# One 512-byte remainder for all large tiles, the attention output split into the buffer of the normed activations, and plain products in the last piece of each MLP, in a two-layer f32 encoder

## The chip, the cores and the metric

The kernel runs on one core of a Trainium2 chip. The metric is device time in microseconds (us) of one execution; a lower time is better. Times before are 1498.27, 1499.73 and 1499.77, median 1499.73.

## The reference

An input `x` of 512 tokens by 1024 goes through two layers. Each layer has a token mixer and an MLP, each behind an RMS norm and added to the residual:

```python
for i in range(DEPTH):                       # DEPTH = 2
    h = rms_norm(x, norm_mix[i])
    if i % 2 == 0:
        y = dilated_mixer(h, a_w_qkv[j], a_q_gain[j], a_k_gain[j], a_w_o[j])
    else:
        y = mla_mixer(h, b_w_in[j], b_q_a_gain[j], b_w_qb[j], b_kv_a_gain[j], b_w_kvb[j], ...)
    x = x + y
    h = rms_norm(x, norm_ffn[i])
    x = x + sq_relu_mlp(h, ffn_w1[i], ffn_w2[i])   # relu(h @ w1)**2 @ w2, 1024 -> 4096 -> 1024
```

Mixer A (layer 0) is windowed attention in three groups of dilation 1, 4 and 16, with 8 heads of 128 each; the three outputs of a head are merged by their softmax denominators, and a 1024 x 1024 output projection follows. Mixer B (layer 1) projects to latents of 256 (queries), 128 (keys and values) and 64 (rotary key), expands them to 8 heads, attends over all 512 tokens and has an output projection of the same size. Everything is f32.

## The kernel before, in words

**Three products for one.** TensorE multiplies in the rounded form fp32r. Each f32 operand is split into a high part (rounded) and a low part (the rest), and a product is the sum of high x high, high x low and low x high. A weight unit of 256 rows by 512 columns comes by DMA from SyncE's queue (SP) into a `raw` tile (3 buffers, line 130); ScalarE copies it to `whi` (L145), VectorE subtracts to get `wlo` (L146), 4 buffers each. Activations are split the same way: `hT` holds the normed activations transposed, high and low, in 32 KB of each partition. Such tiles come from the pool `big` under the tag "hT" (`new_hT`). `run_block` (L149 to L178) is the ordinary block: four accumulators in PSUM, the weight units one after another or all four loaded first, the three products at L172, and a function `evac` for each finished accumulator.

**Stages in order.** Norm of the input; mixer A, two heads at a time; output projection (`project`, L620); MLP; norm; mixer B; projection; MLP; store.

**Mixer A.** For each pair of heads the loop from L436 makes queries, keys and scores (`qk_all`; probabilities are the tiles `P`), values (`v_all`), then `merge` (L364 to L405) and `pv` (L407 to L434). `merge` brings maxima and denominators of the first group into the order of the others by small products with a selection matrix (L374), works out the weights on VectorE and ScalarE, brings them back by another product (L399) and multiplies all `P` tiles with them (L405). `pv` transposes `P` (L117), multiplies with the values (L428, L432) and copies to `oT`. For the last pair the order is values of head 0, `qk_all`, `merge`, values of head 1, `pv` twice.

**Mixer B.** One pair of heads at a time: scores (L829), softmax, transposed probabilities in `pTs` (L845 and its neighbour), value product (`pv_b`, L853) and a ScalarE copy to `oB`. The heads are staggered by three token rows. For the last pair all PSUM tiles come from the pools `sc` and `tp` (`bank`, L734), so that the four accumulators are free.

**Output projection.** `project` splits `oT` or `oB` into two tiles `osp` (L626 to L628, eight copies on ScalarE and eight subtractions on VectorE, after the attention), then multiplies in two halves of 512 columns, 96 products each; in the second half each finished row is normed (`norm_tile`) and its transposed, split form goes to `hT` (L117, L208, L209).

**MLP.** Four pieces of 1024 hidden units. An up block is 96 products (L172); the activations `a2` are f32. A down piece (`wino`, L470) multiplies 2 x 2 blocks with seven block products in place of eight: 7 x 24 = 168 matmuls, with sums and differences of activation blocks (tile `S`) and of weight blocks (tiles `wq`) on VectorE (L493), splits of both (L502 and L503 to `asp`, L509 and L510 to `whi` and `wlo`), and results added to the residual (L545). The order is up(0,0), up(0,1), then for each piece up(ch+1,0), down(ch), up(ch+1,1), and down(3) at the end. `ORDER` and `ORDER_P` list the seven products; the last piece of each MLP uses `ORDER_P`, which finishes rows earlier, and calls `done` after each step: norms in layer 0, stores in layer 1.

**What sets the order.** The program runs under a tile framework whose scheduler reorders each engine's instructions by a simulated timeline, within the dependences; on the chip each engine then runs its list in that order. Pools give the addresses, and a tile of a pool waits until the readers of what stood there are done.

**Addresses.** In the built program the tiles start at these remainders of their byte address in the partition modulo 512:

| tiles | before | after |
|---|---|---|
| hT, raw, whi, wlo, pTs | 192 | 192 |
| oT, oB, the a2 in `x16`, osp, resid, wq, asp, S, mixer A's P of group 0 and its constants | 64 | 192 (osp is gone) |
| mixer A's other tiles (values, keys, tables, pT) | 352 | 192 |
| mixer B: kn, kr, vb | 384 | 192 |
| mixer B: qn, qr, pe | 448 | 192 |
| mixer B: latents cT and rotary tables | 96 | 192 |

Of the kernel before, what the change touches and what calls it, by code (L numbers as in the profile page):

```python
# [10 lines left out]
F32 = mybir.dt.float32  # L11
# [6 lines left out]
P = 128  # L18
# [36 lines left out]


# [29 lines left out]
def encoder_kernel(ctx: ExitStack, tc: tile.TileContext, x, norm_mix, norm_ffn, a_w_qkv, a_q_gain, a_k_gain,  # L86
# [17 lines left out]
    st = ctx.enter_context(tc.tile_pool(name="st", bufs=6))  # L104
    acc_p = ctx.enter_context(tc.tile_pool(name="acc_p", bufs=4, space=PSUM))
# [123 lines left out]
    with tc.tile_pool(name="apool", bufs=1, reuse_waits="tile") as ap_, \  # L229
            tc.tile_pool(name="aw", bufs=2, reuse_waits="tile") as aw, \  # L230
            tc.tile_pool(name="adram", bufs=2, space=bass.MemoryType.DRAM) as ad:
        xts = [aw.tile([P, D], F32, tag="vt", name=nm("xt")) for r in range(2)]
# [8 lines left out]
        ca = ap_.tile([P, C_ALL - C_KEEP], F32, name="ca")  # L241
        gqk = ap_.tile([P, 2, NG * DH], F32, name="gqk")
        load_x(0)
# [24 lines left out]
        cosg, sing = {}, {}  # L268

        def tables(g):  # L270
            eng = V if g == 0 else G
            cg = ap_.tile([P, NT, 2, DH], F32, name=f"cosg{g}")
            sg = ap_.tile([P, NT, 2, DH], F32, name=f"sing{g}")
# [5 lines left out]
            cosg[g], sing[g] = cg, sg  # L279
# [156 lines left out]
        for b in range(HA // 2):  # L436
# [33 lines left out]
    def wino(tag, Aq, w, pool, resid, order, done=None):  # L470
# [29 lines left out]
        def split_a(x):  # L500
            t = pool.tile([P, 4, 2, 256], F32R, tag="asp", name=nm("asp"), bufs=3)
            A.activation(t[:, :, 0], x, AF.Copy)  # L502
            V.tensor_tensor(t[:, :, 1], x, t[:, :, 0].bitcast(F32), op=ALU.subtract)  # L503
            return t

# [7 lines left out]
        def need_t1():  # L513
            if "t1" not in raw:
                sub(b11, b12, b11)
                raw["t1"] = b11

        def operands(p):
            if p == 1:
                return Aq(0, 0), b11  # L520
            if p == 5:
                stmp("c", Aq(1, 0), Aq(1, 1), ALU.add)
                need_t1()
# [8 lines left out]
            if p == 7:  # L532
                stmp("d", Aq(0, 0), Aq(1, 0), ALU.subtract)
                need_t1()
# [13 lines left out]
        for step, (p, chain, first, last, adds) in enumerate(order):  # L548
            a, wq = operands(p)
            at = split_a(a)  # L550
# [394 lines left out]
```

## Time and profile before

| quantity | value |
|---|---|
| median of three runs | 1499.73 us |
| profiled execution | 1500.14 us |
| its span (first to last instruction) | 1498.4 us |
| mean granted TensorE clock | 0.981 of full speed |
| TensorE busy | 1436.6 us, 7116 matmuls |
| VectorE busy | 954.1 us |
| ScalarE busy | 723.6 us |
| GpSimd busy | 176.8 us |
| DMA, mean over the span | 90 GB/s |

The profile is that of one execution. Its own time, 1500.14 us, is 1.7 us more than its span, for what lies ahead of the first and behind the last instruction. Times of stages are read from the span, in us from its start. PE is TensorE, DVE VectorE, ACT ScalarE, POOL GpSimd and SP SyncE; a line number such as L172 is one of the code above. A row of the timeline has start, busy time, engine, line, operation, output and inputs, tile and element counts, and in square brackets an idle time ahead of it with what ended it. "x8" means that so many instructions were put together.

### The profile page before, as it was taken

The page shows a single profiled execution, that of the slowest core. Times are in us where ns is not written, and L with a number is a line of the kernel's source. Part 1 is how long each engine was busy: PE and PEld are TensorE (multiplying, and loading weights), DVE is VectorE, ACT ScalarE, POOL GpSimd, SP SyncE. Part 2 cuts the span into 40 slices and gives each one's busy share as a digit, 9 for nine tenths or more (in the row PEclk, how much of TensorE's full clock was granted, in tenths as well). Part 3 has the DMA queues.
Part 4 walks back from the last instruction along what each step waited for, and adds up shares of the span by engine and source line. Part 5 has one row for each costly group of instructions (what it writes and reads, how often), then busy time and mean ns, then how long its engine had stood idle before and what let it go on. Part 6 is the DMA issues. An engine that isn't in the chain of part 4 may idle for free.

```text
span 1498.4 us, 19268 instructions
## 1 busy us (share of the span) xinstructions
PE 1436.6 (96%) x7116; PEld 1211.0 (81%) x7116; DVE 954.1 (64%) x1386; ACT 723.6 (48%) x1566; POOL 176.8 (12%) x301
## 2 busy tenths in 40 slices
PE   5999999999999799999999997899889999999997
PEld 4889889889988788888888886777668888888885
DVE  5675565656447634484866877587745286675966
ACT  3653455355336423554535444587633453544542
POOL 5210120120012100000000001664300000000000
PEclk9999999999999899999999998899999999999998
DMA  6315214313422334415151501210003515151401
GB/s 224 92 54 154 69 52 134 96 47 90 139 85 81 96 112 149 147 57 154 29 169 43 163 1 41 64 43 29 29 29 111 184 30 168 42 169 56 127 0 56
DMA packets 112334, 135.44 MB, mean 90 GB/s; under 512 B 7409, under 2 KB 71537, under 8 KB 112241
## 3 DMA queue, kind: packets, MB, share of 16 engines
q1 hardware_dynamic: 112240, 134.22, 29.0%
q8 instruction: 56, 0.92, 0.3%
q14 instruction: 38, 0.30, 0.1%
HBM read 130.00 MB, written 4.19 MB: 90 GB/s over the span
## 4 chain that ended last, share of the span: by engine, by line
PE 87%; DVE 7%; ACT 3%; issue 1%; DMA 1%; POOL 1%; SPq 0%; DVEq 0%; ACTq 0%; POOLq 0%
PE acc L172 55%; PE sc L563 10%; PE tp L563 8%; PE tp L117 3%; PE acc L853 1%; PE sc L746 1%; DVE wlo L510 1%; PE acc L829 1%; DVE wlo L146 1%; PE sco L428 1%; DVE resid L545 1%; PE sco L432 1%; PE sc L339 1%; PE acc L563 1%; PE tp L853 1%
## 5 line engine op out<-in xcount | busy, mean ns | idle before, releaser
L172 PE MATMUL acc<-whi,hT 128*128 128x512 f32 (+2 forms) x1344 | 403.2, 376 | 0.7 <-ACT hT L208 0.7
L146 DVE TENSOR_TENSOR wlo<-raw,whi 128x1024 fp32r<-128x1024 f32 (+3 forms) x172 | 198.7, 1162 | 268.0 <-ACT whi L145 261.7
L172 PE MATMUL acc<-hT,whi 128*128 128x512 f32 (+1 forms) x1152 | 321.9, 366 | 2.4 <-DVE resid L639 1.9
L145 ACT ACTIVATE whi<-raw 128x1024 fp32r<-128x1024 f32 (+3 forms) x172 | 171.7, 1001 | 296.3 <-PE acc L172 221.9
L172 PEld LDWEIGHTS acc<-whi,hT 128*128 128x128 f32 x1344 | 248.6, 190 | 30.5 <-ACT hT L208 1.2
L172 PE MATMUL acc<-wlo,hT 128*128 128x512 f32 (+2 forms) x672 | 250.1, 373 | 2.6 <-DVE wlo L146 2.6
L172 PEld LDWEIGHTS acc<-hT,whi 128*128 128x128 f32 x1152 | 208.4, 189 | 37.9 <-DVE resid L639 2.2
L509 ACT ACTIVATE whi<-wq 128x1024 fp32r<-128x1024 f32 x112 | 118.6, 1061 | 193.4 <-PE acc L172 77.8
L172 PE MATMUL acc<-hT,wlo 128*128 128x512 f32 (+1 forms) x576 | 208.1, 365 | 0.0
L510 DVE TENSOR_TENSOR wlo<-wq,whi 128x1024 fp32r<-128x1024 f32 x112 | 136.9, 1222 | 63.6 <-ACT whi L509 62.9
L563 PE MATMUL sc<-whi,asp 128*128 128x512 f32 x480 | 155.1, 395 | 0.0
L172 PEld LDWEIGHTS acc<-wlo,hT 128*128 128x128 f32 x672 | 127.3, 189 | 18.5 <-DVE wlo L146 3.6
L563 PE MATMUL tp<-whi,asp 128*128 128x512 f32 x352 | 118.0, 407 | 10.6 <-DVE asp L503 6.4
L172 PEld LDWEIGHTS acc<-hT,wlo 128*128 128x128 f32 x576 | 108.6, 189 | 17.6
L563 PEld LDWEIGHTS sc<-whi,asp 128*128 128x128 f32 x480 | 90.4, 188 | 21.0
L563 PE MATMUL sc<-wlo,asp 128*128 128x512 f32 x240 | 94.4, 395 | 0.0
L563 PEld LDWEIGHTS tp<-whi,asp 128*128 128x128 f32 x352 | 68.7, 196 | 29.0 <-DVE asp L503 7.9
L172 PE MATMUL acc<-whi,osp 128*128 128x512 f32 x256 | 80.5, 395 | 1.2 <-ACT osp L627 1.2
L493 DVE TENSOR_TENSOR wq<-wq,wq 128x1024 f32<-128x1024 f32 x64 | 77.7, 1222 | 0.9
L563 PE MATMUL tp<-wlo,asp 128*128 128x512 f32 x176 | 71.2, 404 | 0.0
L122 POOL TENSOR_SCALAR rs_v<-qss 128x4 f32<-128x4 f32 (+1 forms) x64 | 22.7, 354 | 396.2 <-ACT junk L291 363.7
L122 POOL TENSOR_SCALAR rs_v<-nss 128x1 f32<-128x1 f32 x16 | 5.3, 330 | 530.5 <-ACT xn L198 530.5
(193 smaller groups left out, 2120.2 us busy)
## 6 DMA issues: line engine op xcount, KB each, us to landing
raw<-in_ffn_w_dram SPq DMA_DIRECT2D x64, 512.0 KB, 3.7
wq<-in_ffn_w_dram SPq DMA_DIRECT2D x64, 512.0 KB, 4.4
raw<-in_a_w_qkv_dram SPq DMA_DIRECT2D x96, 256.0 KB, 3.1
raw<-in_a_w_qkv_dram SPq DMA_DIRECT2D x64, 192.0 KB, 2.8
raw<-in_a_w_o_dram SPq DMA_DIRECT2D x8, 512.0 KB, 4.7
raw<-in_b_w_o_dram SPq DMA_DIRECT2D x8, 512.0 KB, 3.7
xt<-in_x_dram SPq DMA_DIRECT2D x8, 256.0 KB, 5.7
vd<-vt SPq DMA_DIRECT2D x8, 256.0 KB, 3.8
```

The source lines that it names most:

```text
L117: PE.transpose(o, i, ident)
L122: G.tensor_scalar(v[:, :n], ss, 1.0 / dim, EPS, op0=ALU.mult, op1=ALU.add)
L145: A.activation(hi[:, :nk, :n], raw[:, :nk, :n], AF.Copy)
L146: V.tensor_tensor(lo[:, :nk, :n], raw[:, :nk, :n], hi[:, :nk, :n].bitcast(F32), op=ALU.subtract)
L172: PE.matmul(accs[o][:, oc], lhsT=lt, rhs=rt, start=(kt == 0 and p_i == 0 and hv == 0), stop=(kt == total - 1 and p_i == 2), skip_group_che ...
L339: PE.matmul(sc[:, r * P:(r + 1) * P], lhsT=qT[:, r * P:(r + 1) * P], rhs=kT[:, r * P:(r + 1) * P], start=True, stop=True)
L428: PE.matmul(o[:, r * P:(r + 1) * P], lhsT=vt[:, r, g], rhs=pts[g - 1][:, r * P:(r + 1) * P], start=(r == 0 and g == 1), stop=False, skip_g ...
L493: V.tensor_tensor(o[u], x[u], y[u], op=ALU.subtract)
L509: A.activation(hi, x, AF.Copy)
L510: V.tensor_tensor(lo, x, hi.bitcast(F32), op=ALU.subtract)
L563: PE.matmul(bk[t], lhsT=lt, rhs=rt[:, j], start=(first and k == 0 and i == 0), stop=(k == 3 and i == 2), skip_group_check=True)
L853: PE.matmul(o, lhsT=d["v"][:, j, h], rhs=pT[:, j], start=(j == 0), stop=(j == NT - 1))
```

## The change

It has three parts and some consequences.

1. *Remainders.* Small tiles (`gn`, `ssr`, `rqs`) move to a pool `sm` with a pad of 128 f32; the constants `ca` and the tile `kr2` are widened; `ck` and mixer A's tables are allocated in another place. All large tiles then start at remainder 192 (table above).
2. *Attention output.* Its split form now lies in a tile of `big` in the slot of "hT": in mixer A `oA`, taken after the last `v_all`, with the same eight copies and eight subtractions; in mixer B `oB`, into which `pv_b` writes the high part (ScalarE) and the low part (VectorE) straight from PSUM, so that the later copies and subtractions are gone. `pTs` goes to `x16`. The normed activations of the MLPs get tiles of their own (`hT_f0`, `hT_f1`).
3. *Last piece of each MLP.* `down_last` replaces the seven products by an ordinary block of eight: four splits of `a2` and 2 x 96 = 192 products at the line of `run_block`, with the weights loaded and split like all others. Each row and half is finished by itself and calls `done(r, c)`: in layer 0 the norm of row r when its second half is finished, in layer 1 a store. `ORDER_P` is gone.
4. The weights of the inner seven-product pieces lie in one tile `wqs` in the slot of "hT"; `asp` has 4 buffers in place of 3; the two loads of `gn` are issued early on SP's queue.

```diff
+    sm = ctx.enter_context(tc.tile_pool(name="sm", bufs=1))
+    gn = sm.tile([P, 2], F32, name="gn")
+    ssr = sm.tile([P, NT], F32, name="ssr")
+    rqs = [sm.tile([P, NT, 2], F32, name=f"rqs{i}") for i in range(2)]
+    sm.tile([P, PAD], F32, name="pad")
...
+        cas = ap_.tile([P, 1920], F32, name="ca")
+        ca = cas[:, 0:C_ALL - C_KEEP]
...
                 merge(stats, Pt, True)
                 vs.append(v_all(1))
+                oA = new_hT()
...
-                t = pool.tile([P, 2, 512], F32, tag=f"wq{slot}", name=nm("wq"), bufs=2)
+                t = wqs[:, 2 * slot + u]
...
+        wqs = big.tile([P, 8, 2, 512], F32, tag="hT", name=nm("wqs"))
...
+        def down_last(ch):
+            a2 = a2s.pop(ch)
+            at = {}
+            for j in range(2):
+                for i in range(2):
+                    at[i, j] = split_a(a2[:, 4 * j:4 * j + 4, 256 * i:256 * i + 256], pool)
+            def mm(r, kt, hi, lo, hv):
+                t = at[r // 2, kt // 4][:, kt % 4]
+                ah, al = (t[:, c, (r % 2) * P:(r % 2) * P + P] for c in range(2))
+                sl = slice(0, 512)
+                return [(ah, hi, sl), (ah, lo, sl), (al, hi, sl)]
+            for c in range(2):
+                def evac(r, acc, c=c):
+                    sl = resid[:, r, 512 * c:512 * c + 512]
+                    V.tensor_tensor(sl, sl, acc, op=ALU.add)
+                    done(r, c)
+                run_block(w_units(w2[1024 * ch:1024 * ch + 1024, :], 512 * c, 512), [1] * 4 if c == 0 else [4], 512,
+                          mm, evac)
...
-        down(3)
+        down_last(3)
-    def project(oS, w, resid, gain_src, pool, g_name):
+    def project(o_hl, w, resid, gain_src, hT_n, pool, g_name):
...
-        parts = [pool.tile([P, 4, 2, S], F32R, name=nm("osp")) for _ in range(2)]
-        for h in range(8):
-            o_hl = parts[h // 4][:, h % 4]
-            A.activation(o_hl[:, 0], oS[:, h], AF.Copy)
-            V.tensor_tensor(o_hl[:, 1], oS[:, h], o_hl[:, 0].bitcast(F32), op=ALU.subtract)
...
+        for h in range(HA):
+            A.activation(oA[:, h, 0], oT[:, h], AF.Copy)
+            V.tensor_tensor(oA[:, h, 1], oT[:, h], oA[:, h, 0].bitcast(F32), op=ALU.subtract)
+        project(oA, a_w_o[0], resid, norm_ffn[0:1, :].rearrange("o d -> (o d)"), hT, po, "g_ffn0")
...
-                A.activation(oB[:, hh], o, AF.Copy)
+                A.activation(oB[:, hh, 0], o, AF.Copy)
+                V.tensor_tensor(oB[:, hh, 1], o, oB[:, hh, 0].bitcast(F32), op=ALU.subtract)
...
-            oB = x16.tile([P, HB, S], F32, tag="x16", name="oB")
-            pTs = big.tile([P, 2, NT, S], F32, tag="hT", name="pTs")
+            oB = new_hT()
+            pTs = x16.tile([P, 2, NT, S], F32, tag="x16", name="pTs")
```

The scheduler gives TensorE another order at three places. Rows show line, operation, output and inputs, and shape; numbers tell tiles of one name apart.

The first place is the merge of mixer A's last pair of heads. `sc` is the last score, `scm` the merge's small products, `P` the probabilities, `sco` the value product. Before:

```order
L339 MATMUL sc_4666<-qkT_4433 128x128
L374 MATMUL scm_4681<-ca,xsel_4678 128x4 x4
L399 MATMUL scm_4702<-ca,xsel_4678 128x4 x2
L117 MATMUL tp_4858<-ck,P_3774 128x128 x4
L117 MATMUL tp_4865<-ck,P_3776 128x128 x4
L428 MATMUL sco_4886<-pT_4863,vt_3782 128x128
L117 MATMUL tp_4872<-ck,P_3772 128x128 x4
```

After, TensorE has products of the output projection there (`hT_4866` is `oA`, `acc_4995` to `acc_4998` are the projection's four accumulators):

```order
L179 MATMUL acc_4998<-whi_5001,hT_4866 128x512
L179 MATMUL acc_4998<-wlo_5002,hT_4866 128x512
L381 MATMUL scm_4689<-ca,xsel_4686 128x4 x4
L179 MATMUL acc_4995<-whi_5001,hT_4866 128x512 x2
L179 MATMUL acc_4995<-wlo_5002,hT_4866 128x512
```

Some rows on, around the merge's second small product:

```order
L179 MATMUL acc_4998<-wlo_5062,hT_4866 128x512
L179 MATMUL acc_4998<-whi_5061,hT_4866 128x512 x2
L179 MATMUL acc_4998<-wlo_5062,hT_4866 128x512
L406 MATMUL scm_4710<-ca,xsel_4686 128x4 x2
L124 MATMUL tp_4867<-ck,P_3782 128x128 x4
L124 MATMUL tp_4874<-ck,P_3784 128x128 x4
L179 MATMUL acc_4998<-whi_5061,hT_4866 128x512
L124 MATMUL tp_4881<-ck,P_3780 128x128 x4
```

Between the last score and `scm_4710` there were the four small products alone; now 71 products of the projection's first half stand there too.

The second place is the end of the first MLP with its norms (`xn` is a normed row, `acc_7796` an accumulator of mixer B's input projection). Before:

```order
L563 MATMUL sc_7394<-wlo_7705,asp_7685 128x512
L563 MATMUL sc_7394<-whi_7704,asp_7685 128x512
L117 MATMUL tp_7647<-ck,xn_7640 128x128 x4
L117 MATMUL tp_7654<-ck,xn_7640 128x128 x4
L172 MATMUL acc_7796<-whi_7802,hT_7638 128x448
```

After (`acc_7504` is the last row's accumulator, `xn_7558` the first normed row):

```order
L179 MATMUL acc_7504<-whi_7507,asp_7364 128x512
L124 MATMUL tp_7565<-ck,xn_7558 128x128 x4
L124 MATMUL tp_7572<-ck,xn_7558 128x128 x4
L179 MATMUL acc_7504<-wlo_7508,asp_7364 128x512
L179 MATMUL acc_7504<-whi_7507,asp_7364 128x512 x2
```

The transposes of the first row stood behind the last product of the MLP; now they stand among the products of its last row.

The third place is the end of mixer B (`pTs`, `vb`: value product; `pe`: probabilities to be transposed; `kn`, `qn`, `kr`, `qr`: scores). Before:

```order
L853 MATMUL tp_9697<-pTs,vb_9191 128x512 x4
L117 MATMUL tp_9716<-ck,pe_9649 128x128 x4
L829 MATMUL sc_9703<-kn_9189,qn_9552 128x512 x3
L829 MATMUL sc_9703<-kr_9190,qr_9553 128x512 x2
L117 MATMUL tp_9722<-ck,pe_9668 128x128 x4
L117 MATMUL tp_9728<-ck,pe_9687 128x128 x4
L117 MATMUL tp_9734<-ck,pe_9712 128x128 x4
L853 MATMUL tp_9740<-pTs,vb_9191 128x512 x4
L172 MATMUL acc_9772<-whi_9778,osp_9754 128x512
```

After (`hT_7969` is `oB`, `acc_9715` and `acc_9716` are accumulators of the projection):

```order
L179 MATMUL acc_9715<-whi_9750,hT_7969 128x512
L838 MATMUL sc_9550<-kn_9143,qn_9495 128x512 x3
L838 MATMUL sc_9550<-kr_9144,qr_9496 128x512 x2
L124 MATMUL tp_9589<-ck,pe_9521 128x128 x4
L179 MATMUL acc_9715<-whi_9750,hT_7969 128x512
L179 MATMUL acc_9715<-wlo_9751,hT_7969 128x512
```

The projection began behind the last value product; now 84 of the first half's 96 products stand ahead of it, between the scores and transposes of the last pair.

More of the change, by code (lines that the diff above doesn't have):

```diff
@@ L54 @@
 C_KEEP = C_COSA
+PAD = 128
 def shape_constants():
@@ L231, in encoder_kernel @@
             tc.tile_pool(name="adram", bufs=2, space=bass.MemoryType.DRAM) as ad:
+        cosg = [ap_.tile([P, NT, 2, DH], F32, name=f"cosg{g}") for g in range(NG)]
+        sing = [ap_.tile([P, NT, 2, DH], F32, name=f"sing{g}") for g in range(NG)]
         xts = [aw.tile([P, D], F32, tag="vt", name=nm("xt")) for r in range(2)]
@@ L467, in encoder_kernel, with split_a, wino @@
                 pv(b, h, Pt, *vs[h])
-    def wino(tag, Aq, w, pool, resid, order, done=None):
+    def split_a(x, pool):
+        t = pool.tile([P, 4, 2, 256], F32R, tag="asp", name=nm("asp"), bufs=4)
+        A.activation(t[:, :, 0], x, AF.Copy)
+        V.tensor_tensor(t[:, :, 1], x, t[:, :, 0].bitcast(F32), op=ALU.subtract)
+        return t
+    def wino(tag, Aq, w, wqs, pool, resid):
         v = w.rearrange("(k p) c -> p k c", p=P)
@@ L511, in split_w @@
             return hi, lo
[L513 to L516, printed above, removed]
         def operands(p):
@@ L547, in wino @@
         banks = {}
-        for step, (p, chain, first, last, adds) in enumerate(order):
+        for p, chain, first, adds in ORDER:
             a, wq = operands(p)
-            at = split_a(a)
+            at = split_a(a, pool)
             if first:
-                pl, tg = {"a": (sc_p, "sc"), "b": (tp_p, "tp"), "d": (acc_p, "acc") if order is ORDER_P else (tp_p, "tp")}[chain]
+                pl, tg = (sc_p, "sc") if chain == "a" else (tp_p, "tp")
                 banks[chain] = [pl.tile([P, 512], F32, tag=tg, name=nm(tg)) for _ in range(2)]
@@ L607, in down @@
             a2 = a2s.pop(ch)
-            last = ch == 3
             wino(layer * 4 + ch, lambda i, j: a2[:, 4 * j:4 * j + 4, 256 * i:256 * i + 256],
-                 w2[1024 * ch:1024 * ch + 1024, :], pool, resid, ORDER_P if last else ORDER, done if last else None)
+                 w2[1024 * ch:1024 * ch + 1024, :], wqs, pool, resid)
+        def down_last(ch):
[16 more added lines that the diff above has]
+                          mm, evac)
         up(0, 0)
@@ L899, in encoder_kernel @@
                     tail = fresh
+    bh = ctx.enter_context(tc.tile_pool(name="bh", bufs=1, reuse_waits="tile"))
+    hT = bh.tile([P, KD, 2, S], F32R, name="hT_f1")
     with tc.tile_pool(name="po1", bufs=1, reuse_waits="tile") as po:
[L902 removed]
+        project(oB, b_w_o[0], resid, norm_ffn[1:2, :].rearrange("o d -> (o d)"), hT, po, "g_ffn1")
     with tc.tile_pool(name="mlp1", bufs=1, reuse_waits="tile") as mp:
[L905 to L912 removed]
+        mlp(1, ffn_w1[1], ffn_w2[1], hT, resid, mp, lambda r, c: nc.sync.dma_start(
+            out_v[:, r, 512 * c:512 * c + 512], resid[:, r, 512 * c:512 * c + 512]))
 _INS = ['x', 'norm_mix', 'norm_ffn', 'a_w_qkv', 'a_q_gain', 'a_k_gain', 'a_w_o', 'b_w_in', 'b_q_a_gain', 'b_w_qb',
```

65 lines of the change are left out of this document (17 added, 48 removed).

## The prediction

> **What bounds the kernel now.** I read the page first: busy times, the clock in 40 slices, and the chain that ended last.
>
> ```profile
> span 1498.4 us, 19268 instructions
> ...
> PE 1436.6 (96%) x7116; PEld 1211.0 (81%) x7116; DVE 954.1 (64%) x1386; ACT 723.6 (48%) x1566; POOL 176.8 (12%) x301
> ...
> PEclk9999999999999899999999998899999999999998
> ...
> PE 87%; DVE 7%; ACT 3%; issue 1%; DMA 1%; POOL 1%; SPq 0%; DVEq 0%; ACTq 0%; POOLq 0%
> ```
>
> PE carries 87% of the chain. So time can come off in three ways only: fewer products, a shorter product, or fewer holes in PE's row and fewer stretches at a lower clock. The page's 96% hides the holes, so I cut the span into stages and asked for the busy time of each (columns: stretch, its length, then for each engine busy us and instructions, then the granted clock, DMA share, GB/s).
>
> ```profile
> 507.80:533.85 26.05, 17.25 (x107) 15.94 (x108) 13.06 (x31) 9.11 (x27) 0.00 (x0) 0.67 0.36 107
> 607.43:650.98 43.55, 43.55 (x194) 36.06 (x193) 26.34 (x23) 22.40 (x29) 0.00 (x0) 1.00 0.31 97
> 650.98:690.02 39.04, 39.04 (x169) 31.65 (x168) 33.39 (x35) 20.74 (x22) 0.00 (x0) 1.00 0.45 134
> 876.90:924.80 47.90, 42.84 (x169) 33.61 (x168) 40.11 (x43) 22.37 (x26) 2.45 (x4) 0.89 0.07 18
> 924.80:952.88 28.08, 25.09 (x129) 22.56 (x128) 14.55 (x19) 13.00 (x34) 7.60 (x16) 0.94 0.12 34
> 952.88:975.20 22.32, 16.63 (x73) 13.35 (x72) 14.40 (x46) 14.47 (x59) 17.39 (x40) 0.77 0.32 95
> 1071.00:1103.30 32.30, 24.83 (x100) 15.43 (x98) 17.68 (x48) 13.20 (x31) 2.01 (x4) 0.95 0.05 16
> 1446.28:1494.52 48.24, 42.71 (x169) 33.21 (x167) 37.01 (x40) 17.54 (x19) 0.00 (x0) 0.89 0.09 33
> ```
>
> In order they are: merge and last two heads of mixer A; 192 products of up blocks; an inner seven-product piece (168 products); the last piece of the first MLP; its last norms with the input projection of mixer B; mixer B's start; its last two heads; the last piece of the second MLP. The dense stages have a clock of 1.00 and no holes, so there the length gives the price of one 512-column product: 43.55 / 192 = 0.2268 us in an up block, 39.04 / 168 = 0.2324 us in an inner piece. The last pieces have the same 168 products and take 8.9 and 9.2 us more. The two ends of attention have holes too.
>
> **The change part by part.** *Remainders.* Up blocks read hT and whi/wlo, both at remainder 192; the seven-product pieces read asp (64) and whi (192). Same shape, same clock, 0.0056 us apart. A second pair with different remainders is osp (64) with whi (192), from the chain in order of time:
>
> ```profile
> 534.13 39.27 PE acc L172 x169
> ```
>
> 39.27 / 169 = 0.2324, the mixed price again. After the change all of these stand at 192. Six inner pieces: 6 x 168 x 0.0056 = 5.6 us; two output projections: 2 x 192 x 0.0056 = 2.1. Sum **7.7 us**, all on PE's path. The low end is 0 (something other than the remainder may make the difference), the high end 8.5 (some 130 score products at 384 against 448 gain likewise). VectorE's splits don't care: the weight split below takes 1229 ns with all operands at 192 and 1222 ns with its source at 64, so I count nothing there.
>
> ```profile
> L146 DVE TENSOR_TENSOR wlo<-raw,whi 128x1024 fp32r<-128x1024 f32 x128 | 156.4, 1229 | 226.5 <-ACT whi L145 220.3 <-DMA v0c<-vd 5.7
> L510 DVE TENSOR_TENSOR wlo<-wq,whi 128x1024 fp32r<-128x1024 f32 x112 | 136.9, 1222 | 63.6 <-ACT whi L509 62.9
> L209 DVE TENSOR_TENSOR hT<-tp,hT 128x512 fp32r<-128x512 f32 x32 | 21.4, 686 | 20.2 <-ACT hT L208 20.1
> L145 ACT ACTIVATE whi<-raw 128x1024 fp32r<-128x1024 f32 x128 | 135.0, 1059 | 257.3 <-PE acc L172 195.3 <-PE sc L563 18.8 <-PE tp L563 15.0
> ```
>
> A rule speaks against this term. The Trainium skill, "TensorE: Matmul & The Clock Gate", Step-by-step, says that TensorE reads weights and moving data through two independent SBUF ports, so that a weight load takes nothing from the running product. By it remainders would change nothing and the sum would lack the 7.7 us; the two prices above are this case's evidence for a difference, though not for its cause.
>
> *Last piece of each MLP.* It goes from 7 to 8 x 24 = 192 products: 24 more, 5.4 us each time. Against that the waits of the old last piece go, and the slow clock behind them:
>
> ```profile
> 901.50 0.51 PE L563 MATMUL tp<-whi,asp 128*128 128x512 f32 x1 [2.09 <-ACT asp L502]
> ...
> 907.63 1.22 PE L563 MATMUL tp<-whi,asp 128*128 128x512 f32 x2 [2.97 <-DVE asp L503]
> ```
>
> ```profile
> 902.40:912.40 10.00, 7.03 (x17) 5.09 (x16) 7.45 (x9) 1.83 (x2) 0.00 (x0) 0.50 0.00 0
> ```
>
> PE waits there for sums of activations and weights that VectorE makes (40.11 of 47.90 us busy), and then runs 10 us at half clock. The new piece is an ordinary block: no sums, eight weight splits, four splits of a2, eight adds, or 8 x 1.23 + 4 x 1.22 + 8 x 0.69 = 20.2 us of VectorE. I price it like 192 up-block products, 43.55 us: 47.90 - 43.55 = 4.3 and 48.24 - 43.55 = 4.7, **9.0 us**. What covers its start: products 0 to 3 of the inner dimension need only the first half of a2, which is old; the second half is needed two weight units (48 products, 10.9 us) later and costs two splits on each engine, under 5 us. If that cover fails, up to 1.5 us each: 6.0 to 9.0.
>
> *Norms at the end of the first MLP.* Rows 0 and 1 of the tokens are now normed while the products of rows 2 and 3 run, since each is finished by itself.
>
> ```profile
> 926.56 0.47 PE L172 MATMUL acc<-whi,hT 128*128 128x448 f32 x1 [0.70 <-ACT hT L208]
> ...
> 929.53 1.11 PE L117 MATMUL tp<-ck,xn 128*128 128x128 f32 x4 [2.29 <-DVE hT L209]
> ```
>
> The stage has 28.08 - 25.09 = 3.0 us of holes, and the granted clock of 0.94 costs at most 0.06 x 28.08 = 1.7. Of 4.7 I take **3.7** (2 to 4.7). In the next stage two of four transposes of the latent rows now stand ahead of the last products; of its 22.32 - 16.63 = 5.7 us of holes I take **1.0** (0 to 4).
>
> *Output projection of mixer A under the merge.* The split output now has a buffer as soon as the last products of the normed input are over, so PE's order puts 71 of the first half's 96 projection products between the scores and the merge's second product. Rows of before:
>
> ```profile
> 507.86 1.05 PE L374 MATMUL scm<-ca,xsel 128*128 128x4 f32 x8 [0.56 <-DVE P L344]
> 515.98 0.98 PE L399 MATMUL scm<-ca,xsel 128*128 128x4 f32 x4 [7.06 <-DVE xsel L394]
> ...
> 528.58 1.04 PE L117 MATMUL tp<-ck,P 128*128 128x128 f32 x8
> ...
> 533.89 0.47 PE L172 MATMUL acc<-whi,osp 128*128 128x512 f32 x1
> ```
>
> ```profile
> 519.04 2.35 DVE L405 TENSOR_TENSOR P<-P,me 128x1024 f32<-128x1024 f32 x2
> ```
>
> What PE needs there: 2.0 us for the merge, and for each head what the second took at full clock, 533.89 - 528.58 = 5.3. So 26.05 - 2.0 - 10.6 = 13.4 us are holes or half clock (0.67 granted). The 71 products last 16.1 us. The merge's chain was 8.1 us (507.86 to 515.98) and gets two weight splits and some five splits of the output put into it on VectorE (2 x 1.23 + 5 x 0.69 = 5.9), 14.0 together: still under 16.1, so the merge is hidden. Not hidden are the two multiplications of 2.35 us that follow its second product. **11.0** us (6 to 13.4). If the cover were gone, the 5.9 us would be on the path.
>
> *Split in mixer B's heads, projection under its end.* Each head adds a VectorE subtraction from PSUM (nearest row: L209, 686 ns) behind the copy that was there; the 16 later copies and subtractions go. In PE's order the projection's products stand between the scores of the last pair.
>
> ```profile
> 1079.22 0.94 PE L829 MATMUL sc<-kn,qn 128*128 128x512 f32 x3
> ...
> 1080.47 0.60 PE L117 MATMUL tp<-ck,pe 128*128 128x128 f32 x4
> ...
> 1087.40 3.59 PE L853 MATMUL tp<-pTs,vb 128*128 128x512 f32 x8
> 1090.83 0.60 PE L117 MATMUL tp<-ck,pe 128*128 128x128 f32 x4
> 1091.19 0.94 PE L829 MATMUL sc<-kn,qn 128*128 128x512 f32 x3
> ...
> 1096.72 5.40 PE L853 MATMUL tp<-pTs,vb 128*128 128x512 f32 x8 [0.69 <-ACT pTs L845]
> 1103.32 0.50 PE L172 MATMUL acc<-whi,osp 128*128 128x512 f32 x1 [1.21 <-ACT osp L627]
> ```
>
> PE needs in 1071.0 to 1103.3: eight scores of 1.25 us (1079.22 to 1080.47), eight sets of transposes of 0.36 (1090.83 to 1091.19), two value products of 3.43 (1087.40 to 1090.83), 0.7 of the head before and some 0.9 of query transposes: 21.4 us. So 10.9 are holes or half clock (the second value product took 5.40 for 3.59). 84 projection products (19.1 us) fill them, all but the last chain: 0.69 for the probabilities, 1.21 for the high half and 0.69 for the low half. 10.9 - 2.6 = **8.3** (4 to 10.9).
>
> *Moved DMAs and buffers, at nothing.* Two tiny gain loads now stand on SP's queue ahead of weights of the second block, not needed for a block's length. The first load of wqs waits for the last projection product, with weights of the second up block queued behind it on SP; these are needed 21.8 us later (half of 43.55) and land in 3.7 (below). Cover gone: one landing each.
>
> ```profile
> raw<-in_ffn_w_dram SPq DMA_DIRECT2D x64, 512.0 KB, 3.7
> ...
> raw<-in_a_w_o_dram SPq DMA_DIRECT2D x8, 512.0 KB, 4.7
> ```
>
> *Sum:* 7.7 + 9.0 + 3.7 + 1.0 + 11.0 + 8.3 = 40.7 us. The profiled execution took 1500.14 us (1.7 outside its span), so 1459.4; it lies 0.4 above the median of the three runs, 1499.73. Forecast **1459.0**.
>
> **Rivals.** *Remainders are not the cause.* For it: the two prices come from different stages, with VectorE busier in the pieces (33.39 of 39.04 us against 26.34 of 43.55). Against: the output projection has the mixed price with VectorE nearly idle. 1459.0 + 7.7 = 1466.7. The port rule of the Trainium skill ("TensorE: Matmul & The Clock Gate", Step-by-step) would have it so.
>
> *The fill is taken back.* In both attention ends VectorE and ScalarE now split the projection's weights between the steps of the softmax; if the chains lengthen by what PE gains and only a third of 19.3 us is left (6.4), 1459.0 + 12.9 = 1471.9. For it: at mixer B's end the scores wait for ScalarE and VectorE already. Against: VectorE is busy 17.68 of 32.30 us, and five splits and two subtractions add 7.5.
>
> *Slower: the projection's weights are late.* PE's order is fixed, so a projection product that waits for its weights holds back the merge or score behind it. If each of the eight weight units of the two early halves is loaded and split only when it is due, each costs 4.7 + 1.06 + 1.23 = 7.0 us, 56 in all, and the time is 1459.0 + 56 = 1515. It is slower than before from six such units on (40.7 / 7.0 = 5.8). Against: four split buffers each, and loads that are queued early.
>
> **How the numbers follow.** Forecast 0.74, remainders not the cause 0.10, fill taken back 0.11, late weights 0.05. The range takes in the forecast's bounds and both middle rivals: the best ends sum to 8.5 + 9.0 + 4.7 + 4 + 13.4 + 10.9 = 50.5, or 1449; the upper end is 1472. A measurement here tells 0.2% (3 us) from no change: faster 0.94, same 0.01, slower 0.05 (the late weights).
>
> **What would show it.** Inner pieces of 38.1 us and projections at 0.227 us a product prove the remainders; 39.0 disproves them. Last pieces of 43.5 to 45 us with clock 1.00. No idle of 7 us before the merge's second product, and PE's slices there at full clock. First value products of the last pair surrounded by projection products without waits over 1 us. The forecast is wrong if PE waits for whi or wlo at either projection, or if score waits in the last pair grow.

## The result and the profile after

The changed kernel takes 1457.94 us (median of four runs, 1456.11 to 1458.84) against 1499.0 for the kernel before on the same chip (1497.34 to 1499.77): ratio 0.9726, 95% interval 0.9709 to 0.9743. The profiled execution took 1457.66 us. The forecast was 1459.0.

From the page of the changed kernel, the span, the busy times, the granted clock in 40 slices and the chain that ended last:

```profile
span 1455.6 us, 19232 instructions
...
PE 1420.5 (98%) x7164; PEld 1207.9 (83%) x7164; DVE 892.6 (61%) x1324; ACT 702.1 (48%) x1540; POOL 176.1 (12%) x301
...
PEclk9999999999999999999999999999999999999999
...
PE 92%; DVE 3%; DMA 2%; ACT 1%; POOL 1%; issue 1%; SPq 0%; ACTq 0%; POOLq 0%; DVEq 0%
```

There are 48 matmuls more, and this span is 42.8 us shorter than the one before (1498.4 - 1455.6); the medians differ by 41.1. The slices below 9 in the clock's row are gone.

The stages that the prediction spoke of, in the changed kernel (stretch, length, busy us and instructions of PE, PEld, DVE, ACT and POOL, granted clock, DMA share, GB/s): merge and last two heads of mixer A with the projection products among them; an up block; an inner seven-product piece; the last piece of the first MLP with the first row's transposes; the norms with the input projection of mixer B; the last two heads of mixer B; the last piece of the second MLP.

```profile
507.58:539.13 31.55, 29.17 (x183) 25.72 (x182) 19.21 (x38) 10.84 (x28) 0.00 (x0) 1.00 0.51 173
594.86:638.40 43.54, 43.54 (x194) 36.04 (x193) 27.25 (x24) 23.43 (x30) 0.00 (x0) 1.00 0.31 97
638.40:676.48 38.08, 38.08 (x169) 31.53 (x168) 32.12 (x34) 19.78 (x21) 0.00 (x0) 1.00 0.45 137
861.44:905.89 44.45, 44.45 (x201) 36.82 (x200) 19.76 (x21) 15.61 (x21) 9.46 (x15) 1.00 0.19 57
905.89:928.63 22.74, 22.74 (x127) 21.03 (x126) 13.61 (x27) 11.90 (x32) 5.25 (x13) 1.00 0.36 95
1041.05:1086.50 45.45, 44.08 (x193) 31.98 (x192) 24.86 (x57) 18.86 (x41) 4.45 (x8) 1.00 0.15 47
1408.25:1451.77 43.52, 43.52 (x193) 35.85 (x191) 13.12 (x14) 8.42 (x10) 0.00 (x0) 1.00 0.19 67
```

The inner piece has the price of an up block now: 38.08 / 168 = 0.2267 us a product. The last pieces have no hole, and VectorE is busy for less than half of them.

To see where the 42.8 us of the two profiled spans come from, I cut both spans at the same events: the start of mixer A's last scores, the first up product of the first MLP, the start of its last piece, the last value product of mixer B's third pair, the first up product of the second MLP, and the start of its last piece. Four of these stretches in the kernel before, and below it the same in the changed one:

```profile
506.25:580.75 74.50, 64.95 (x326) 54.69 (x325) 36.45 (x60) 23.76 (x49) 2.24 (x6) 0.89 0.29 93
876.92:1068.70 191.78, 174.87 (x829) 138.43 (x828) 144.75 (x317) 121.03 (x356) 74.51 (x155) 0.94 0.13 37
1068.70:1150.35 81.65, 73.91 (x315) 54.28 (x313) 41.34 (x77) 31.47 (x61) 5.95 (x13) 0.98 0.11 33
1150.35:1446.30 295.95, 294.80 (x1384) 246.07 (x1385) 194.90 (x189) 140.94 (x166) 0.74 (x2) 1.00 0.34 109
```

```profile
504.37:568.03 63.66, 59.75 (x325) 50.36 (x325) 36.48 (x60) 23.68 (x48) 2.24 (x6) 1.00 0.33 108
861.44:1041.05 179.61, 171.70 (x849) 137.72 (x848) 122.92 (x293) 111.62 (x346) 73.95 (x154) 0.98 0.18 54
1041.05:1113.73 72.68, 70.96 (x317) 53.86 (x316) 38.03 (x72) 27.84 (x55) 6.70 (x14) 1.00 0.12 37
1113.73:1408.25 294.52, 292.19 (x1385) 245.73 (x1385) 188.88 (x185) 141.35 (x166) 0.74 (x2) 1.00 0.33 106
```

| stretch | gain, us | forecast for it, us |
|---|---|---|
| start to mixer A's last scores (506.25 - 504.37) | 1.9 | 0 |
| end of mixer A and its projection | 10.8 | 11.0 + 1.1 (remainders) |
| up blocks and inner pieces of the first MLP | 2.8 | 2.8 |
| its last piece, norms, mixer B up to its third pair | 12.2 | 4.3 + 3.7 + 1.0 |
| end of mixer B and its projection | 9.0 | 8.3 + 1.1 |
| up blocks and inner pieces of the second MLP | 1.4 | 2.8 |
| its last piece and the end | 4.7 | 4.7 |
| sum | 42.8 | 40.8 (40.7 there, by rounding) |

The 1.9 us at the top are mostly no part of the change: at 31 us one set of four transposes and twelve products took 4.8 us in the kernel before and 3.3 in the changed one, and in five of the ten experiments, which do the same work there as the changed kernel, it took 4.8 or 4.9 again, in the others 3.3.

### The profile page after: what moved, and what is told of

It reads as the page before. It is cut to its first block, busy times and chain, and to the rows that moved or that the text cites. A ratio compares the mean times of both kernels' runs of the same rounds, so it can differ in the third digit from the quotient of the medians.

```text
span 1455.6 us, 19232 instructions
## 1 busy us (share of the span) xinstructions
PE 1420.5 (98%) x7164; PEld 1207.9 (83%) x7164; DVE 892.6 (61%) x1324; ACT 702.1 (48%) x1540; POOL 176.1 (12%) x301
## 4 chain that ended last, share of the span: by engine, by line
PE 92%; DVE 3%; DMA 2%; ACT 1%; POOL 1%; issue 1%; SPq 0%; ACTq 0%; POOLq 0%; DVEq 0%
PE acc L179 63%; PE sc L566 9%; PE tp L566 7%; PE tp L124 4%; PE acc L862 1%; PE acc L838 1%; PE sc L755 1%; PE sco L439 1%; PE sco L435 1%; PE sc L346 1%; DMA raw<-in_ffn_w_dram 1%; PE sc L838 1%; PE acc L124 1%; PE sc L339 0%; PE tp L862 0%
## 5 line engine op out<-in xcount | busy, mean ns | idle before, releaser
L179 PE MATMUL acc<-whi,hT 128*128 128x512 f32 (+2 forms) x1600 | 485.4, 378 | 2.1 <-ACT hT L659 1.2
L179 PE MATMUL acc<-hT_f,whi 128*128 128x512 f32 (+1 forms) x1152 | 321.9, 366 | 1.9 <-DVE resid L645 1.4
L179 PEld LDWEIGHTS acc<-hT_f,whi 128*128 128x128 f32 x1152 | 208.3, 189 | 37.6 <-DVE resid L645 1.8
L179 PE MATMUL acc<-hT_f,wlo 128*128 128x512 f32 (+1 forms) x576 | 208.2, 366 | 0.4 <-DVE wlo L153 0.4
L518 ACT ACTIVATE whi<-wqs 128x1024 fp32r<-128x1024 f32 x84 | 89.1, 1061 | 110.2 <-PE sc L566 42.6
L179 PEld LDWEIGHTS acc<-hT_f,wlo 128*128 128x128 f32 x576 | 108.6, 189 | 18.0 <-DVE wlo L153 0.6
L519 DVE TENSOR_TENSOR wlo<-wqs,whi 128x1024 fp32r<-128x1024 f32 x84 | 102.6, 1222 | 26.0 <-ACT whi L518 25.8
L179 PE MATMUL acc<-whi,asp 128*128 128x512 f32 x256 | 78.9, 389 | 0.0
L131 POOL TENSOR_TENSOR qrs<-rs_v,nhalf 128x4 f32<-128x4 f32 (+1 forms) x64 | 65.8, 1027 | 5.3 <-POOL rs_v L129 0.2
L298 ACT ACTIVATE junk<-acc 128x128 f32<-128x128 f32 x192 | 53.0, 276 | 23.1 <-PE acc L179 16.2
```

What stands on the lines that cost most here:

```text
L131: G.tensor_tensor(r[:, :n], v[:, :n], nhalf[:, :n], op=ALU.pow)
L179: PE.matmul(accs[o][:, oc], lhsT=lt, rhs=rt, start=(kt == 0 and p_i == 0 and hv == 0), stop=(kt == total - 1 and p_i == 2), skip_group_che ...
L298: A.activation(junk, a4[:, c], AF.Square, accum_out=ss[:, c:c + 1])
L518: A.activation(hi, x, AF.Copy)
L519: V.tensor_tensor(lo, x, hi.bitcast(F32), op=ALU.subtract)
```

## The experiments

All start from the changed kernel, whose profiled span of 1455.6 us and stretches above are what they are compared with. The ratios are to the kernel before, run on the same chip.

**Offsets of one operand.** Each piece of an MLP gets another distance, in bytes, between the split activations `asp` and the weights; views move inside a wider buffer (`off` counts f32, so 16 are 64 bytes), and the instructions and their order stay as they are.

```diff
-        t = pool.tile([P, 4, 2, 256], F32R, tag="asp", name=nm("asp"), bufs=4)
+        off = (16, 32, 48, 112, 64, 80, 96, 8)[piece]
+        t = pool.tile([P, 2176], F32R, tag="asp", name=nm("asp"), bufs=4)
+        t = t[:, off:off + 2048].rearrange("p (k c n) -> p k c n", k=4, c=2)
```

> The changed kernel with the split activations asp of each MLP piece moved inside a wider buffer: pieces 0, 1, 2 of the first MLP by 64, 128, 192 bytes, of the second by 256, 320, 384, the last piece of the first MLP by 448, of the second by 32. Weights (whi, wlo) stay at remainder 192; the order of work on TensorE is the same. Theory (the price of a product depends on the remainder of the stationary tile against the moving one): the piece moved by 384, which is the distance of the kernel before (64 against 192), has 0.2324 us a product, 39.04 us for 168; what the other distances cost is open, between 0.2267 and 0.2324 us. Rival (remainders are not the cause; VectorE's load in the old kernel, or the place in memory, was): all inner pieces keep 38.08 us, 0.2267 a product.

The six inner pieces in order (distances 64, 128, 192, 256, 320, 384), the first 169 products of the first MLP's last piece (448), and the whole last piece of the second (32):

```profile
639.64:678.84 39.20, 39.20 (x170) 31.58 (x168) 32.30 (x34) 19.80 (x21) 0.00 (x0) 1.00 0.42 134
722.39:761.43 39.04, 39.04 (x170) 31.66 (x168) 32.27 (x34) 19.77 (x21) 0.00 (x0) 1.00 0.42 134
804.95:843.40 38.45, 38.45 (x169) 31.55 (x168) 33.29 (x35) 20.71 (x22) 0.00 (x0) 1.00 0.09 26
1189.50:1227.58 38.08, 38.08 (x169) 31.53 (x168) 32.12 (x34) 19.79 (x21) 0.00 (x0) 1.00 0.43 137
1271.10:1310.30 39.20, 39.20 (x170) 31.58 (x168) 32.29 (x34) 19.79 (x21) 0.00 (x0) 1.00 0.45 134
1353.85:1392.89 39.04, 39.04 (x170) 31.65 (x169) 33.41 (x35) 20.72 (x22) 0.00 (x0) 1.00 0.09 26
...
865.16:903.84 38.68, 38.68 (x170) 31.69 (x169) 15.50 (x16) 10.73 (x14) 8.69 (x13) 1.00 0.22 66
1414.65:1459.45 44.80, 44.80 (x193) 35.88 (x191) 13.13 (x14) 8.43 (x10) 0.00 (x0) 1.00 0.18 65
```

At a clock of 1.00 and with much the same load on VectorE, only the place of `asp` differs, while the weights stay at 192, and it sets the price. By the distance to the weights it is 39.20 us at 64 and again at 320, 39.04 at 128 and at 384, 38.45 at 192, 38.08 at 256, as at 0. At 448 a product costs 38.68 / 169 = 0.2289 us, what 192 has (38.45 / 168); at 32 it costs 44.80 / 192 = 0.2333, what 64 has (39.20 / 168). So the price repeats after 256 bytes, not 512, and none of the distances tried is cheaper than 0. The rival that VectorE made the difference falls: it is busy 32.3 us in the dearest and 32.1 in the cheapest piece. The kernel took 1465.39 us (one run).

**Everything moved by 256 bytes.** A tile of 64 f32 stands ahead of all others.

```diff
+    cpool.tile([P, 64], F32, name="shift")
```

> The changed kernel with 256 bytes put ahead of all tiles, so that every large tile stands at 448 in place of 192. Theory (only the distance between the two operands counts): inner pieces 38.08 us, up blocks 43.52 us, time within 3 us of 1458. Rival (the remainder itself counts, 192 is a good one): 0.0056 us more for each of some 5000 products of 512 or 256 columns, 20 us or more.

1458.01 us (one run). The first inner piece:

```profile
639.27:677.35 38.08, 38.08 (x170) 31.53 (x168) 32.12 (x34) 19.78 (x21) 0.00 (x0) 1.00 0.42 137
```

The place 192 has no merit of its own beside 448. Since the price repeats after 256 bytes in the run above, this shift can't tell an absolute place with that period from a distance; a shift of all tiles by 64 or 128 bytes was not run, so this half of the question stays open.

**One remainder undone.** `off` is 96 (384 bytes) in all eight pieces, the old distance of `asp`.

> The changed kernel with asp of all eight pieces moved by 384 bytes, to remainder 64 as in the kernel before; all else at 192, same order of work on TensorE. Theory: (6 x 168 + 2 x 192) x 0.0056 = 7.8 us more than the changed kernel, inner pieces 39.04 us, last pieces 0.2324 us a product; about 1465.7, ratio to before 0.978. Rival (remainders are not the cause): no change, 1458.

1465.95 us (1465.43 to 1466.33), ratio 0.9792 (0.9776 to 0.9808); 8.0 us more than the changed kernel's median, 7.8 expected. An inner piece:

```profile
638.50:677.53 39.03, 39.03 (x169) 31.66 (x168) 32.27 (x34) 19.76 (x21) 0.00 (x0) 1.00 0.44 135
```

**No fill at the end of mixer A.** The projection takes the heads from the last pair to the first.

```diff
+            def mm(r, kt, hi, lo, hv):
+                return act_stationary(o_hl, 512)(r, 6 - kt + 2 * (kt % 2) if back else kt, hi, lo, hv)
-            run_block(w_units(w, 512 * c, 512), [1, 1, 1, 1] if c == 0 else [4], 512, act_stationary(o_hl, 512), evac)
+            run_block(w_units(w, 512 * c, 512)[::-1 if back else 1], [1, 1, 1, 1] if c == 0 else [4], 512, mm, evac)
```

> The changed kernel with the heads of mixer A's output projection taken from the last pair to the first (6, 7, 4, 5, ...), so that its first product needs the value product of head 6 and the projection can't fill the merge. Same instructions, same buffers. Theory: the fill is what was gained there; the time from the start of the last scores (504.37 us in the changed kernel) to the first up product of the MLP (568.03) grows from 63.7 to 73.4 us (74.5 in the kernel before, less 192 x 0.0056 for the remainders), 9.7 us more, about 1467.5. Rival (the early buffer or the split lying ahead of the projection brought it, not the order on TensorE): under 3 us more.

1468.88 us (1468.17 to 1469.75), ratio 0.9803 (0.9786 to 0.9819). The stretch, and from the timeline the merge's two small products:

```profile
505.54:581.70 76.16, 63.91 (x325) 54.13 (x325) 36.42 (x60) 23.70 (x48) 2.24 (x6) 0.89 0.29 91
```

```profile
507.15 1.05 PE L381 MATMUL scm<-ca,xsel 128*128 128x4 f32 x8 [0.56 <-DVE P L351]
516.99 0.98 PE L406 MATMUL scm<-ca,xsel 128*128 128x4 f32 x4 [8.79 <-DVE xsel L401]
```

12.5 us more than with the fill (76.16 - 63.66), where 9.7 were expected. The idle time and the clock of 0.89 are back, so the order on TensorE is the cause. The median grew by 10.9 us only, since in this run the scheduler also changed the order in mixer B, which took 2.1 us less (110.30 us from the first product with the latents to the third pair, against 112.42). The wait ahead of the second small product is 1.7 us longer than in the kernel before (8.79 against 7.06), since the splits of the attention output now stand in the merge's chain; the fill covers that too.

**Less fill at the end of mixer B.** The same edit at the other projection.

> The changed kernel with the heads of mixer B's output projection taken from the last pair to the first, so that the projection can't stand between the scores of the last pair. Theory: from the last value product of the pair before (1041.05 us in the changed kernel) to the first up product (1113.73) 72.7 us become 80.6 (81.65 in the kernel before, less 1.07 for the remainders), 7.9 us more, about 1465.8. Rival (the split written straight from PSUM, which is kept, brought it): under 2 us more.

1459.5 us (1459.11 to 1460.26), ratio 0.9742 (0.9728 to 0.9757). The stretch:

```profile
1040.51:1116.41 75.90, 72.08 (x318) 53.60 (x317) 38.08 (x73) 28.05 (x55) 6.70 (x14) 1.00 0.12 36
```

Only 3.2 us more instead of 7.9, between the two theories. But twelve products of head 6 still stood ahead of the last value product, in a place where the kernel before has waits of 1.93 and 0.69 us close together. So I took these away too. The first of the two waits, in the kernel before:

```profile
1095.40 0.63 PE L117 MATMUL tp<-ck,pe 128*128 128x128 f32 x4 [1.93 <-DVE pe L836]
```

**No fill at the end of mixer B.** The heads run strictly backwards, also inside a weight unit.

```diff
-                        for j in range(nk):
+                        for j in range(nk)[::-1 if back else 1]:
```

> The changed kernel with mixer B's projection taking the heads strictly backwards (7, 6, 5, ...), so that not one of its products can stand ahead of the last value product; in the run before with 6, 7, 4, ... twelve products of head 6 still stood there. Theory (those twelve lay in the costliest hole, ahead of the last value product, and kept the clock up): from the last value product of the pair before to the first up product 75.9 us become about 80.6. Rival (the low half written straight from PSUM in the heads, in place of the block of 16 operations behind them, brought what was left): under 77 us.

1464.15 us (1463.55 to 1465.45), ratio 0.9774 (0.9758 to 0.9791). The stretch, and below it 3.41 us of the last value product, from 0.40 us behind its start; then from the timeline the last transposes and that product, here and, below it, with the twelve products:

```profile
1040.68:1120.45 79.77, 73.99 (x318) 54.20 (x317) 37.98 (x73) 28.10 (x55) 6.71 (x14) 0.98 0.10 34
1068.87:1072.28 3.41, 3.41 (x5) 1.35 (x4) 0.00 (x0) 0.00 (x0) 0.00 (x0) 0.50 0.02 5
```

```profile
1067.16 0.63 PE L124 MATMUL tp<-ck,pe 128*128 128x128 f32 x4 [1.96 <-DVE pe L848]
1068.47 5.40 PE L865 MATMUL tp<-pTs,vb 128*128 128x512 f32 x8 [0.69 <-ACT pTs L857]
```

```profile
1066.60 1.18 PE L179 MATMUL acc<-whi,hT 128*128 128x512 f32 x4
1067.61 0.60 PE L124 MATMUL tp<-ck,pe 128*128 128x128 f32 x4
1068.90 3.70 PE L864 MATMUL tp<-pTs,vb 128*128 128x512 f32 x8 [0.69 <-ACT pTs L856]
```

The whole fill is worth 79.77 - 72.68 = 7.1 us, and 3.9 of them hang on twelve products of 0.227 us: they fill the wait of 1.96 us, and the value product behind runs at full clock, 3.70 us in place of 5.40 with 3.41 us of it at 0.50. The other 72 bring 3.2. These shares hold for this order of taking away, the 72 first; the other order was not run.

**Norms asked for late.** In the first MLP the four rows are normed at the call for the last row.

```diff
-            norm_tile(r, resid[:, r], state["g"], state["hT"], mp, xn_tag="S")
+            if r == 3:
+                for q in range(4):
+                    norm_tile(q, resid[:, q], state["g"], state["hT"], mp, xn_tag="S")
```

> The changed kernel, but the four rows are normed only when the last row of the first MLP is finished. Theory (the early norms gained more than the 3.7 + 1.0 us forecast): from the start of the last piece (861.44) to the first product with the latents (928.63) 67.2 us become about 73, 5 to 6.6 us more. Rival (only the products of the last piece gained, the norms are hidden by the rows that are left): under 2 us more.

1462.53 us (one run), and only 1.0 more in the stretch:

```profile
862.04:930.23 68.19, 67.68 (x328) 57.72 (x326) 33.04 (x44) 27.20 (x53) 15.07 (x28) 1.00 0.23 65
```

That looked like the rival. But the edit doesn't do what it says: the scheduler still puts the scaling of the first two rows (`xn`) on VectorE at 894.8 and 898.8 us, ahead of the last product at 905.3. It tells nothing of late norms.

**Rows that finish together.** This takes away what lets rows finish early: in the first MLP the weight units of the second half go over all four rows in turn.

```diff
-                run_block(w_units(w2[1024 * ch:1024 * ch + 1024, :], 512 * c, 512), [1] * 4 if c == 0 else [4], 512,
-                          mm, evac)
+                run_block(w_units(w2[1024 * ch:1024 * ch + 1024, :], 512 * c, 512),
+                          [1] * 4 if c == 0 or layer == 0 else [4], 512, mm, evac)
```

> The changed kernel with the weight units of the second half of the first MLP's last piece taken one after the other over all four rows, so that the four rows finish within the last 48 products in place of one after the other. The number of products is the same. Theory (rows that finish one by one let their norms run early, and that carries the gain behind the last piece): the chain of one norm (add, square, power, scaling, transposes, split) stands bare between the last product and mixer B's input projection; from the start of the last piece to the first product with the latents 67.2 us become 72 to 74. Rival (VectorE, freed of the sums of the seven products, carries it): under 69 us.

1463.4 us (one run). The stretch up to the first product with the latents, the one up to mixer B's third pair, and TensorE's waits behind the last product:

```profile
861.01:933.17 72.16, 69.57 (x327) 58.82 (x325) 32.90 (x44) 27.18 (x53) 16.02 (x28) 0.98 0.22 62
...
861.01:1047.67 186.66, 174.92 (x849) 139.69 (x848) 122.82 (x293) 111.34 (x346) 74.28 (x154) 0.96 0.17 52
```

```profile
905.45 1.09 PE L124 MATMUL tp<-ck,xn 128*128 128x128 f32 x8 [0.76 <-DVE xn L207]
...
909.05 0.66 PE L124 MATMUL tp<-ck,xn 128*128 128x128 f32 x4 [1.58 <-DVE hT L216]
```

5.0 us more (72.16 - 67.19) in the first of the two. In the kernel before it took 78.09 us:

```profile
876.92:955.01 78.09, 68.69 (x304) 56.72 (x302) 55.80 (x66) 36.52 (x65) 11.94 (x25) 0.91 0.11 29
```

So 10.9 us were gained there, 4.3 of them in the last piece, and of the other 6.6 this run loses 5.0. VectorE is as free here as in the changed kernel (32.90 us busy against 33.37), so it is the early finish of rows that carries most of that gain. Up to the third pair 7.0 us are lost (186.66 - 179.61), but the 2.1 of mixer B's stages can't be put down to late norms alone: the scheduler gave them another order than in the changed kernel, the same as in the run with the norms asked for late, which loses 1.7 us there too (114.09 us against 112.42).

**Seven products in the last pieces.** `down(3)` works by `ORDER_P` again, with the old calls of `done` for norms and stores; all operands stand at one remainder.

```diff
-        down_last(3)
+        down(3)
```

> The changed kernel with the seven-product last piece in both MLPs, in its old order, with all operands at remainder 192. Theory: its waits come back, less 168 x 0.0056 for the remainders: the last piece of the second MLP takes 47.2 us to its last product in place of 43.3, that of the first about 3.5 more, and the norms behind it 5 to 6.6 more; 12 to 14 us more, about 1471. Rival (the waits came from the mixed remainders or from the buffers of that kernel): last pieces of 38 to 40 us, and a time under 1455.

1472.91 us (1471.9 to 1474.29), ratio 0.9832 (0.9817 to 0.9846). The last piece of the first MLP, the norms with mixer B's input projection, and the last piece of the second MLP; then the two largest waits in the latter:

```profile
860.79:908.65 47.86, 42.48 (x170) 33.36 (x168) 40.96 (x43) 22.24 (x26) 11.71 (x13) 0.93 0.07 20
908.65:937.50 28.85, 25.71 (x136) 23.08 (x134) 16.27 (x28) 13.60 (x36) 7.09 (x15) 0.94 0.14 36
1420.56:1468.15 47.59, 42.23 (x169) 33.17 (x167) 37.02 (x40) 17.52 (x19) 0.00 (x0) 0.89 0.09 33
```

```profile
1444.95 0.50 PE L572 MATMUL tp<-whi,asp 128*128 128x512 f32 x1 [2.09 <-ACT asp L480]
...
1451.19 1.22 PE L572 MATMUL tp<-whi,asp 128*128 128x512 f32 x2 [3.22 <-DVE asp L481]
```

15.0 us more, 12 to 14 expected. In the profiled execution the first last piece with its norms took 9.5 us more and the second 4.1, as expected; another 2.6 lie in mixer B, where the order on TensorE is that of the run before. The cheaper products bring nothing here (47.86 us against 47.90 in the kernel before): the waits shown are for splits that follow VectorE's sums (VectorE is busy for 40.96 of 47.86 us), so TensorE waits a little longer for them.

**A step further.** Of the two multiplications behind the merge's second product, the second head's goes to GpSimd.

```diff
-                    V.tensor_tensor(t, t, ev[:, g, h].unsqueeze(2).broadcast_to(list(t.shape)), op=ALU.mult)
+                    (G if both and g == 0 and h else V).tensor_tensor(
+                        t, t, ev[:, g, h].unsqueeze(2).broadcast_to(list(t.shape)), op=ALU.mult)
```

> An attempt to go on from the changed kernel: of the two multiplications of 1.2 us behind the merge's second product, that of the second head goes to GpSimd, so that VectorE copies the first transposes 1.2 us earlier and the idle time of 2.09 us ahead of the third set of transposes shrinks. Theory: from the start of the last scores to the first up product 63.7 us become 62.5; about 1456.5. Rival (GpSimd takes over 5 us for it, and the second head waits for it): 64 us or more.

1454.19 us (1453.78 to 1454.99), ratio 0.9707 (0.9693 to 0.9722): the shortest of all kernels here. The interval of its ratio overlaps the changed kernel's, which ran on another occasion; the two ranges of runs don't overlap. The stretch from the last scores, the wait that was 2.09 us, and the operation on GpSimd:

```profile
505.17:567.66 62.49, 59.73 (x325) 50.34 (x324) 35.76 (x59) 23.69 (x48) 5.17 (x7) 1.00 0.34 111
```

```profile
526.22 0.66 PE L124 MATMUL tp<-ck,P 128*128 128x128 f32 x4 [0.95 <-DVE pT L422]
```

```profile
524.39 2.93 POOL L412 TENSOR_TENSOR P<-P,me 128x1024 f32<-128x1024 f32 x1 [32.52 <-DVE me L407]
```

Here 1.2 us are gained, as expected. Another 3.7 come from mixer B, whose order the scheduler changed though the edit doesn't touch it: from the first product with the latents to the third pair it takes 108.73 us in place of 112.42, at a clock of 1.00 in place of 0.97; the other stretches of this execution took 2.5 us more. So the larger part is luck: nothing in the edit aims at it. Five of the ten experiments got another order in that stretch and took 108.73 to 115.05 us for it; with the changed kernel's order six executions took 111.09 to 112.42.

## Why the prediction was right

That the sum came so close is partly luck. Against the stretches the terms were 3.2 us too low at the norms with mixer B's start, and 1.3, 0.4 and 1.4 us too high at mixer A's end, mixer B's end and the second MLP; the 1.9 us at the top were in no term.

**Remainders, 7.7 us.** Right in size and in place. The inner pieces gained 0.96 each (39.04 to 38.08), mixer A's projection has the low price too (33 products from 552.02 to 559.50 us, 0.2267 each), undoing `asp` alone costs 8.0 us, and the rival of another cause falls with the offsets. The remainder modulo 512 was too fine a measure: the price repeats after 256 bytes. One argument for this term was misread: VectorE is not nearly idle in the old output projection, but busy for 17.04 of 39.27 us; and there are 160 score products, not some 130, which adds 0.2 us to the upper bound. The port rule of the Trainium skill ("TensorE: Matmul & The Clock Gate", Step-by-step) left no room for such a price; these runs have up to 0.0067 us a product (39.20 against 38.08 for 168), and the measurement decides. They don't show where in the chip the two operands meet.

**Last pieces, 9.0 us.** Right: without holes they take the price of an up block, and with seven products the old length comes back at equal remainders. The gain on the second one is 4.7 us, as forecast.

**Norms and mixer B's start, 3.7 + 1.0 us.** The mechanism was right, the size too small. The stretch gained 12.2 us in all, 7.9 without the last piece's 4.3: 6.6 up to the first product with the latents, 1.3 behind it. The prediction had put some of the holes ahead of the latents into the term for mixer B's start and taken 1.0 of 5.7 us there. With rows that finish together 5.0 of the 6.6 us are lost again. What the 1.3 come from stays open, since mixer B's time changes by more than that with the scheduler's order.

**Mixer A's fill, 11.0 us.** 9.8 measured (10.8 less 1.1 for the remainders). The step on what is late next held: behind the second small product TensorE waits 2.09 us for VectorE.

```profile
526.57 0.66 PE L124 MATMUL tp<-ck,P 128*128 128x128 f32 x4 [2.09 <-DVE pT L421]
```

The clock is not safe around this wait: in the runs with the offsets and with all tiles moved by 256 bytes, 3.41 us with a granted clock of 0.50 fall there (from 527.43 and from 525.57), and the stretch takes 65.28 and 65.05 us in place of 63.66. Against a kernel with the same split, but no fill, the fill is worth 12.5.

**Mixer B's fill, 8.3 us.** 7.1 by the run without any, 7.9 by the stretch. The step that took the holes as one sum, filled by 84 products, was too coarse: with the other 72 gone, 12 products bring over half.

**At nothing.** Nothing shows that the moved loads cost anything. But the stretch from the second MLP's first product to its last piece gained 1.4 us, not the 2.8 of the remainders: TensorE's idle time in it grew from 1.2 us (295.95 - 294.80) to 2.3 (294.52 - 292.19), of which 1.35 are one wait for the norms behind mixer B's projection, where the longest before was 0.93. Some of the difference is spread: in the eight experiments that don't move `asp` it took 293.16 to 295.37 us.

```profile
1116.64 0.65 PE L124 MATMUL tp<-ck,xn 128*128 128x128 f32 x4 [1.35 <-DVE hT_f L216]
```

**Rivals.** Late weights did not occur: at neither projection does TensorE wait for `whi` or `wlo`, and in mixer B's last pair its waits are two of 0.69 us, ahead of the last value product and behind it. "The fill is taken back" had a true part: the splits lengthen the merge's chain by 1.7 us, but behind products that hide it.

## What to carry to other kernels

Compare the price of one product between stages of equal shape at full clock: a difference of 2.5% was worth 8 us here, and moving one tile by some bytes removed it. Look for waits that stand close together ahead of dense work, since they can also cost clock behind them; a dozen products there did more than six dozen elsewhere. An edit that only asks for a later step proves nothing under a scheduler that reorders: take away what lets the step be early. And see in each run whether the stages that the edit doesn't touch have kept their order; here another order moved one of them by up to 3.7 us.

## What the runs showed of the hardware

- A product of 512 columns costs 0.2267 us at a distance of 0 or 256 bytes between its operands' places in a partition, 0.2289 at 192 and 448, 0.2324 at 128 and 384, and 0.2333 at 32, 64 and 320. The weights stood at 192 each time, so a place of the other operand with that period would give the same prices.
- Waits of 1.96 and 0.69 us with 0.6 us of transposes between them were followed, from 0.40 us into the value product on, by 3.41 us at a granted clock of 0.50, and the product took 5.40 us against 3.70; in the kernel before waits of 1.93 and 0.69 us had the same effect. A wait of 2.07 us that ended at 1077.60 there, between denser work, did not: the 2.9 us behind it ran at 1.00.
- While GpSimd multiplied `P` (2.93 us from 524.39), a VectorE subtraction that began at 526.69 took 1.72 us:

```profile
526.69 1.72 DVE L153 TENSOR_TENSOR wlo<-raw,whi 128x1024 fp32r<-128x1024 f32 x1
```

It usually takes 1.21 to 1.23, and it ended 1.08 us after GpSimd. The same is found without that edit, in the changed kernel, where the split starts 0.25 us behind a GpSimd operation of 0.91 us and also ends 1.08 us after it:

```profile
24.67 0.91 POOL L285 TENSOR_TENSOR cosg<-ca,gqk 128x256 f32<-128x256 f32 x1
24.92 1.74 DVE L153 TENSOR_TENSOR wlo<-raw,whi 128x1024 fp32r<-128x1024 f32 x1
```

Two more there, at 1028.23 and 1042.80, take 1.27 and 1.34 us and end 1.08 us after a GpSimd operation that was under way. The Trainium skill ("SBUF — State Buffer", SBUF: two separate sides) says that a VectorE operation with two SBUF inputs and a GpSimd operation that reads SBUF lock each other out of a shared port, and whichever starts first keeps it to its end. That fits these rows; no run here was made to test it.
